# A decoder trunk on one core: both parts of x in one MLP product, and the first norm's high parts straight from the transposed bank

## The chip, the core and the metric

The kernel runs on one core of one Trainium2 chip. The metric is the device time of one execution in microseconds (us). One execution is profiled; its trace gives the rows below. Engines: TensorE (PE; its weight loads are PEld), VectorE (DVE), ScalarE (ACT), GpSimd (POOL) and SyncE (SP), which issues most transfers.

## What is computed

Two layers (`DEPTH = 2`) over 256 rows of 1024 columns, all in float32. The mixer (three groups of attention heads and gates) is untouched by the change. What is touched is the norm ahead of the first layer and the MLP:

```python
h = _layer_norm(x, ln_in_g, ln_in_b)
for l in range(DEPTH):
    mix = _hybrid_mixer(h, ...)
    h = _layer_norm(ALPHA * h + mix, ln1_g[l], ln1_b[l])
    ffn = _conv_gated_mlp(h, w_up[l], conv_w[l], conv_b[l], w_down[l])
    h = _layer_norm(ALPHA * h + ffn, ln2_g[l], ln2_b[l])

def _conv_gated_mlp(x, w_up, conv_w, conv_b, w_down):   # D_FF = 2816
    gate, val = jnp.split(x @ w_up, 2, axis=-1)
    gate = causal_depthwise_conv(gate, conv_w) + conv_b  # width 3, along the rows
    return (jax.nn.silu(gate) * val) @ w_down
```

## The kernel before

**Products in two parts.** TensorE multiplies in the type fp32r. To keep float32 accuracy each operand is split into a high part (ScalarE copies it to fp32r) and a low part (VectorE subtracts the high part from the full value), and each product is three matmuls: high by high, low by high, high by low (`mm3`).

**Weights.** `Stream` brings the weights in the order of `stream_plan` through the SP queue into seven `raw` tiles; `split` makes of each piece a tile `hl` of two parts (16 buffers): ScalarE the high part, VectorE or GpSimd the low part. `take` and `free` hand the tiles to the products in order.

**Order.** All instructions are issued in the order in which the program is written (a manual schedule). `Tasks` holds generators for the side work; `tick`, called after nearly each group of matmuls, moves each one step on, and `refill` splits the next weight piece. `Clocks` keeps a rough model of the engines' times, and `ready` and `refill` decide by it, so that the order of the side work depends on the model. All instructions go through one helper; their line in the trace is L276 (L281 in the changed kernel).

**PSUM.** Four banks `acc` for accumulators and four banks `att` for the rest. `get_att` and `att` hand out the latter in a ring; `att_free` gives back in the order of the program.

**The start.** `first_norm(tb, ...)` runs for rows 0 to 127 (tb 0) and 128 to 255 (tb 1). For each half of the columns (q) TensorE transposes four blocks into one `att` bank, and VectorE multiplies by the gain and adds the bias in the bank (`gb` holds both, one column for each block of 128). `spins` are matmuls on a constant that keep TensorE running. Then `split_out` makes the high part hTh (ScalarE, a whole bank) and the low part hTl (VectorE, a whole bank). `unit_x_tbfirst` then computes the q projection, one block of rows after the other, `evac` copies its two `acc` banks with ScalarE, rotary passes of VectorE follow, and TensorE transposes the result.

**The MLP.** hT is two tiles, hTh and hTl, of 8 blocks by 256 columns. An up unit j makes 256 columns of the gate and 256 of the up half in two `att` banks, G and V: `unit_w` goes through 8 weight tiles of 512 columns with four times three matmuls of 256 columns each. `task_act` then convolves G (ScalarE `cv<-att,convp` with scale and bias, VectorE four passes that read the bank), applies Silu, multiplies with V (VectorE `cv<-cv,att`) and splits the result into `act`. Unit j=0 is computed by rows (`up0`) and transposed into its G and V by `task_first`. A down unit is 24 matmuls of 512 columns into four `acc` banks; the last two down units are done at the end, one block of rows after the other, with the norm of each half behind it (`ln_half`).

Of the kernel before, what the change touches and what calls it, by code (L numbers as in the profile page):

```python
# [76 lines left out]
def stream_plan():  # L77


    plan = []  # L80

    def add(n, kts, cols=512, k0=0):
        step = 2 if cols <= 512 else 1
        for k in range(k0, k0 + kts, step):
            plan.append((n, k, step, cols))

    add("bq", 8)
    add("g1", 8, NG1)
    for n in ("biq", "cq", "ck", "cv", "aq", "ak", "av"):
        add(n, 8)  # L90
    for b in (1, 0):
        for nh in range(2):
            add(f"gate{b}{nh}", 8)
            add(f"br{b}{nh}", 4)
    for nh in range(2):
        add(f"gate2{nh}", 8)
    for nh in range(2):
        add(f"br2{nh}", 4)
    for k0 in (0, 4):
        for nh in range(2):  # L100
            add(f"out{nh}", 4, 512, k0)
    downs = {j: [j - 1] for j in range(1, NPAIR)}
    downs[NPAIR - 2] = []
    downs[NPAIR - 1] = [NPAIR - 3, NPAIR - 2, NPAIR - 1]
    for j in range(NPAIR):
        add(f"up{j}", 8)
        for d in downs.get(j, []):
            add(f"down{d}", 2, 1024)
    return plan, downs


class Stream:


    def __init__(self, nc, ve, sc, clocks, flat, raw_pool, hl_pool, plan):
# [6 lines left out]
        for (_, _, kts, cols) in plan:  # L122
# [4 lines left out]
            w = 512 if cols >= 512 else cols  # L127
# [68 lines left out]
def part(x):  # L196

    return x.name + "low" if x.name[:2] == "hl" and x.offset % 1024 >= 512 else x.name
# [126 lines left out]
def tile_hybrid(ctx: ExitStack, tc: tile.TileContext, a: dict, out: bass.AP):  # L325
# [273 lines left out]
    def first_norm(tb, st, hT, flag):  # L599
# [13 lines left out]
        for q in range(2):  # L613
# [4 lines left out]
            v = bk.rearrange("p (k t) -> p k t", k=4)  # L618
            for i, f in enumerate((ALU.mult, ALU.add)):
                ve.tensor_tensor(v, v, gb[:, i, 4 * q:4 * q + 4].unsqueeze(2).broadcast_to([P, 4, P]), f)  # L620
        spins((9, 5)[tb])
        if tb:
            att_free(warm)
        for q, bk in enumerate(bks):
            split_out(hT[0][:, 4 * q:4 * q + 4, tb * P:(tb + 1) * P],
                      hT[1][:, 4 * q:4 * q + 4, tb * P:(tb + 1) * P],
                      bk.rearrange("p (k t) -> p k t", k=4))
            att_free(bk)
            if not tb and not q:
                W.split(gp)  # L630
# [64 lines left out]
    def unit_w(hT, bks):  # L695

        for k in range(KD):
            w = W.take()
            for i in range(4):
# [6 lines left out]
                if i % 2:  # L706
                    T.tick()
            W.free()
# [16 lines left out]
    def layer(l, hT, hflag):  # L725
# [524 lines left out]
        def task_act(j, G, V):  # L1250
# [10 lines left out]
            att_free(G)  # L1261
# [3 lines left out]
            att_free(V)  # L1265
# [17 lines left out]
        for j in range(NPAIR):  # L1283
# [3 lines left out]
            G, V = get_att(), get_att()  # L1287
            unit_w(hT1, [G, V])
            T.add(task_act(j, G, V))
# [18 lines left out]
        for tb in range(2):  # L1308
            ts = slice(tb * P, (tb + 1) * P)
            st = small([P, 2, 6], "bst")  # L1310
            for i, (nh, c0, c1) in enumerate(PIECES):
                W.hold = W.hold or nh == 1
                for d in (NPAIR - 2, NPAIR - 1):
                    T.until(lambda: d in acts)
                    for f in range(2):
                        w = ws[d, f, nh][:, :, c0:c1]
                        mm3(dacc[nh][tb][:, c0:c1], acts[d][:, 0, f, ts], acts[d][:, 1, f, ts],
                            w[:, 0, :], w[:, 1, :], False, d == NPAIR - 1 and f == 1)
                        if tb and c1 == 512:
                            W.free()  # L1320
                        if True:
                            T.tick()
                if not (tb and nh and l < DEPTH - 1):
                    ln_half(tb, nh, st, dacc[nh][tb], (c0, c1), i)
# [18 lines left out]
    for _ in range(3):  # L1343
# [35 lines left out]
def lay_out(inp):  # L1379
# [3 lines left out]
    for l in range(DEPTH):  # L1383
# [9 lines left out]
        for j in range(NPAIR):  # L1393
            mats[f"up{j}"] = np.concatenate([inp["w_up"][l][:, 256 * j:256 * j + 256],
                                             inp["w_up"][l][:, D_FF + 256 * j:D_FF + 256 * j + 256]], axis=1)
# [34 lines left out]
```

## Time and profile before

| | |
|---|---|
| runs | 913.07 us, median of 3 (912.96 to 913.5) |
| the profiled execution | 913.03 us; its span in the trace 911.2 us |
| mean granted clock of TensorE | 0.997 of 2.4 GHz |
| TensorE busy | 898.0 us, 99% of the span |
| VectorE busy | 652.1 us, 72% |
| ScalarE busy | 512.1 us, 56% |
| GpSimd busy | 46.4 us, 5% |
| read from HBM | 159.47 MB, 176 GB/s over the span |

The span runs from the first to the last event that the profiler took; the execution's own time is 1.8 us longer. Matmuls overlap their neighbours in a row, so the time of one is read from the starts of rows, not from the busy column.

### The profile page before, as it was taken

The page shows a single profiled execution, that of the slowest core. Times are in us where ns is not written, and L with a number is a line of the kernel's source. Part 1 is how long each engine was busy: PE and PEld are TensorE (multiplying, and loading weights), DVE is VectorE, ACT ScalarE, POOL GpSimd, SP SyncE. Part 2 cuts the span into 40 slices and gives each one's busy share as a digit, 9 for nine tenths or more (in the row PEclk, how much of TensorE's full clock was granted, in tenths as well). Part 3 has the DMA queues.
Part 4 walks back from the last instruction along what each step waited for, and adds up shares of the span by engine and source line. Part 5 has one row for each costly group of instructions (what it writes and reads, how often), then busy time and mean ns, then how long its engine had stood idle before and what let it go on. Part 6 is the DMA issues. An engine that isn't in the chain of part 4 may idle for free. (4 is left out here: it accounts for less than half of the span.)

```text
span 911.2 us, 14459 instructions
## 1 busy us (share of the span) xinstructions
PE 898.0 (99%) x5334; PEld 786.7 (86%) x5334; DVE 652.1 (72%) x1272; ACT 512.1 (56%) x1008; POOL 46.4 (5%) x65
## 2 busy tenths in 40 slices
PE   8999999999999999999999999999999999999996
PEld 5878998888888999999888789888888899999995
DVE  6789576966778766666787966775757876766655
ACT  5664766655527555555365556775554475555540
POOL 5100000011010000000000000000200100000000
PEclk9999999999999999999999999999999999999998
DMA  8736253867537665655453335566675376666501
GB/s 300 278 94 205 73 185 116 303 203 242 167 102 273 213 188 182 191 187 177 130 170 137 99 115 162 185 207 211 198 241 183 127 262 188 174 198 187 175 11 47
DMA packets 46680, 161.47 MB, mean 177 GB/s; under 512 B 5840, under 2 KB 6864, under 8 KB 46608
## 3 DMA queue, kind: packets, MB, share of 16 engines
q1 hardware_dynamic: 44208, 155.20, 52.7%
q0 software_dynamic: 1408, 4.98, 2.0%
q8 instruction: 42, 0.69, 0.3%
q10 hardware_dynamic: 992, 0.35, 0.2%
q14 instruction: 30, 0.25, 0.1%
HBM read 159.47 MB, written 1.05 MB: 176 GB/s over the span
## 5 line engine op out<-in xcount | busy, mean ns | idle before, releaser
L276 DVE TENSOR_TENSOR hl<-raw,hl 128x512 fp32r<-128x512 f32 (+1 forms) x580 | 388.4, 695 | 183.3 <-ACT hl L276 181.7
L276 ACT ACTIVATE hl<-raw 128x512 fp32r<-128x512 f32 (+1 forms) x584 | 347.5, 628 | 189.4 <-PE att L276 95.2
L276 PE MATMUL acc<-hl,hTh 128*128 128x512 f32 (+1 forms) x896 | 274.7, 388 | 2.4 <-ACT hTh L276 2.3
L276 PE MATMUL att<-hTh,hl 128*128 128x256 f32 x1280 | 231.5, 283 | 0.0
L276 PEld LDWEIGHTS att<-hTh,hl 128*128 128x128 f32 x1280 | 200.8, 192 | 1.4
L276 PEld LDWEIGHTS acc<-hl,hTh 128*128 128x128 f32 x896 | 166.5, 188 | 38.8 <-ACT hTh L276 4.5
L276 PE MATMUL att<-hTl,hl 128*128 128x256 f32 x640 | 181.1, 283 | 0.0
L276 PE MATMUL acc<-hl,hTl 128*128 128x512 f32 (+1 forms) x448 | 164.8, 385 | 0.1
L276 PE MATMUL acc<-hl,act 128*128 128x512 f32 x528 | 123.1, 390 | 0.0
L276 PEld LDWEIGHTS att<-hTl,hl 128*128 128x128 f32 x640 | 122.8, 192 | 0.0
L276 PEld LDWEIGHTS acc<-hl,act 128*128 128x128 f32 x528 | 98.0, 188 | 19.6
L276 PEld LDWEIGHTS acc<-hl,hTl 128*128 128x128 f32 x448 | 83.9, 188 | 17.0 <-DVE hTl L276 1.8
L276 PE MATMUL acc<-hl,oT 128*128 128x512 f32 x288 | 68.4, 391 | 0.0
L276 PEld LDWEIGHTS acc<-hl,oT 128*128 128x128 f32 x288 | 53.6, 188 | 10.8
L276 DVE SCALAR_TENSOR_TENSOR cv<-att,convp,cv 128x255 f32<-128x255 f32 x88 | 40.4, 479 | 16.1 <-ACT cv L276 14.5
L276 PE MATMUL acc<-hTh,hl 128*128 128x256 f32 x256 | 48.0, 288 | 0.0
L276 PE MATMUL acc<-hl,mT 128*128 128x512 f32 x192 | 44.9, 391 | 0.0
L276 PEld LDWEIGHTS acc<-hl,mT 128*128 128x128 f32 x192 | 35.7, 188 | 7.2
L276 PEld LDWEIGHTS acc<-hTh,hl 128*128 128x128 f32 x256 | 39.8, 191 | 1.5 <-issue 1.3
L276 PE MATMUL acc<-hTl,hl 128*128 128x256 f32 x128 | 36.2, 283 | 0.0
L276 POOL TENSOR_TENSOR rs<-mv,mhalf 128x1 f32<-128x1 f32 x10 | 9.5, 948 | 485.0 <-DVE mv L276 485.0
L276 ACT ACTIVATE t<-acc 128x512 f32<-128x512 f32 (+1 forms) x36 | 20.1, 586 | 21.6 <-PE acc L276 20.8
(166 smaller groups left out, 680.3 us busy)
## 6 DMA issues: line engine op xcount, KB each, us to landing
raw<-in_w_dram SPq DMA_DIRECT2D x284, 512.0 KB, 4.2
raw<-in_w_dram SPq DMA_DIRECT2D x8, 332.0 KB, 4.0
lng<-in_ln_g_dram POOLq DMA_DIRECT2D x4, 512.0 KB, 4.4
lnb<-in_ln_b_dram POOLq DMA_DIRECT2D x4, 512.0 KB, 6.3
h<-in_x_dram SPq DMA_DIRECT2D x4, 256.0 KB, 4.2
lng<-in_ln_in_g_dram SPq DMA_DIRECT2D x1, 512.0 KB, 7.7
lnb<-in_ln_in_b_dram SPq DMA_DIRECT2D x1, 512.0 KB, 8.8
wu<-in_w_ukv_dram POOLq DMA_DIRECT2D x2, 256.0 KB, 5.3
```

The source lines that it names most:

```text
L276: f(*args, **kw)
```

## The change

**MLP.** hT becomes one tile of [128, 8, 2, 256], so that the high and low parts of a block lie side by side. `unit_w2` runs, for each weight block, one matmul of 512 columns (high weight by both parts) and one of 256 (low weight by the high part) into the left half of the bank. The two halves of a bank are then added: `task_sum` copies the left half to SBUF with ScalarE (tile `gv`) and adds the right half with VectorE. A bank now holds 128 columns of the gate or of the up half, so a unit is two halves (f = 0, 1) with two banks each, and the weights of `up{j}` (j from 1) are laid out in two pieces `up{j}.0` and `up{j}.1` of four blocks by 256 columns. `task_act` reads `gv` instead of the banks. Unit j=0 and the down units keep their form.

**First norm.** VectorE's two passes over the bank and the split are replaced: for each block of 128 columns ScalarE makes the high part straight from the bank, with gain and bias as scale and bias of the same instruction, and VectorE makes the full value from the bank; behind the four blocks VectorE subtracts once. The spins go from 9 and 5 to 3 and 3; of the weight splits at the start, two (before three) come ahead and two (before one) stand between the two banks.

**End of a layer.** The last sixteen weight tiles are taken pair by pair (d outer, halves of the columns inner) instead of half by half.

The diff, cut:

```diff
     def new_hT():
-        return (hp.tile([P, KD, S], R32, name=nm("hTh"), tag="hTh"),
-                hp.tile([P, KD, S], R32, name=nm("hTl"), tag="hTl"))
+        t = hp.tile([P, KD, 2, S], R32, name=nm("hT"), tag="hT")
+        return t[:, :, 0, :], t[:, :, 1, :], t
...
             transpose4(bk, h[tb][q])
-            v = bk.rearrange("p (k t) -> p k t", k=4)
-            for i, f in enumerate((ALU.mult, ALU.add)):
-                ve.tensor_tensor(v, v, gb[:, i, 4 * q:4 * q + 4].unsqueeze(2).broadcast_to([P, 4, P]), f)
-        spins((9, 5)[tb])
+        spins((3, 3)[tb])
         if tb:
             att_free(warm)
         for q, bk in enumerate(bks):
-            split_out(hT[0][:, 4 * q:4 * q + 4, tb * P:(tb + 1) * P],
-                      hT[1][:, 4 * q:4 * q + 4, tb * P:(tb + 1) * P],
-                      bk.rearrange("p (k t) -> p k t", k=4))
+            full = t2([P, 4, P])
+            for k in range(4):
+                i = 4 * q + k
+                g, b = gb[:, 0, i:i + 1], gb[:, 1, i:i + 1]
+                sc.activation(hT[0][:, i, tb * P:(tb + 1) * P], bk[:, k * P:(k + 1) * P], AF.Identity,
+                              bias=b, scale=g)
+                ve.tensor_scalar(full[:, k, :], bk[:, k * P:(k + 1) * P], g, b, ALU.mult, ALU.add)
             att_free(bk)
+            ks = slice(4 * q, 4 * q + 4)
+            ve.tensor_tensor(hT[1][:, ks, tb * P:(tb + 1) * P], full,
+                             hT[0][:, ks, tb * P:(tb + 1) * P].bitcast(F32), ALU.subtract)
             if not tb and not q:
-                W.split(gp)
+                for _ in range(2):
+                    W.split(gp)
...
+    def unit_w2(hT, bks):
+        for k in range(0, KD, 2):
+            w = W.take()
+            for kk in range(2):
+                for i in range(2):
+                    c = kk * 256 + i * P
+                    mm(bks[i], w[:, 0, c:c + P], hT[2][:, k + kk, :, :], k + kk == 0, False)
+                    mm(bks[i][:, 0:S], w[:, 1, c:c + P], hT[0][:, k + kk, :], False, k + kk == KD - 1)
+                T.tick()
+            W.free()
...
+        def task_pair(j, gv, done):
+            while len(done) < 2:
+                yield
+            yield from task_act(j, gv[:, 0, :], gv[:, 1, :], False)
+
+        def task_sum(gv, f, bks, done):
+            yield from ready("ACT", *bks)
+            for q, bk in enumerate(bks):
+                o = gv[:, q, f * S:f * S + S]
+                sc.activation(o, bk[:, 0:S], AF.Copy)
+                ve.tensor_tensor(o, o, bk[:, S:], ALU.add)
+                att_free(bk)
+            done.append(f)
...
-            G, V = get_att(), get_att()
-            unit_w(hT1, [G, V])
-            T.add(task_act(j, G, V))
+            gv = t4([P, 2, 512], n="gv")
+            done = []
+            for f in range(2):
+                bks = [get_att(), get_att()]
+                unit_w2(hT1, bks)
+                T.add(task_sum(gv, f, bks, done))
+            T.add(task_pair(j, gv, done))
...
-            for i, (nh, c0, c1) in enumerate(PIECES):
-                W.hold = W.hold or nh == 1
-                for d in (NPAIR - 2, NPAIR - 1):
-                    T.until(lambda: d in acts)
+            for d in (NPAIR - 2, NPAIR - 1):
+                T.until(lambda: d in acts)
+                for nh in range(2):
+                    W.hold = W.hold or (nh == 1 and d == NPAIR - 1)
...
-    for _ in range(3):
+    for _ in range(2):
         W.split(gp)
```

How the order of instructions changes is shown at three places. In the rows that follow, names carry the number of their tile: `hl8` is the ninth weight tile, `att_8` a bank of the pool; a name with its own number behind it is only its identity. What a row waits for stands in brackets.

**First place: ScalarE in the norm of rows 0 to 127, at the start of the program.** `hT` and `hTh` are the transposed rows, `raw` the weights as loaded. Before:

```order
L276 ACTIVATE hl0_175<-raw0_106 128x512 [waits DMAHW6_49]
L276 ACTIVATE hl1_178<-raw0_106 128x512
L276 ACTIVATE hl2_183<-raw1_108 128x512 [waits DMAHW7_49]
L276 ACTIVATE hTh_2_162<-att_8_186 128x4x128 [waits DVE_49,PE_49]
L276 ACTIVATE hl3_211<-raw1_108 128x512
L276 ACTIVATE hTh_2_162<-att_9_193 128x4x128 [waits DVE_49,PE_49]
```

And now:

```order
L281 ACTIVATE hl0_174<-raw0_106 128x512 [waits DMAHW6_49]
L281 ACTIVATE hl1_177<-raw0_106 128x512
L281 ACTIVATE hT_2_162<-att_7_182,gb_97 128x128 [waits DMAHW2_49,PE_49]
L281 ACTIVATE hT_2_162<-att_7_182,gb_97 128x128 [waits DVE_49] x3
L281 ACTIVATE hl2_205<-raw1_108 128x512 [waits DMAHW7_49]
L281 ACTIVATE hl3_208<-raw1_108 128x512
L281 ACTIVATE hT_2_162<-att_8_187,gb_97 128x128 [waits PE_49]
L281 ACTIVATE hT_2_162<-att_8_187,gb_97 128x128 [waits DVE_49] x3
```

Each copy of a whole bank has become four pieces of 128 columns; the second to fourth of a bank wait for VectorE, and the splits of `raw1` stand between the two banks.

VectorE at the same place (`bst` are the stats of rows 128 to 255). Before:

```order
L276 TENSOR_TENSOR att_8_186<-att_8_186,gb_97 128x512 [waits DMAHW2_49,PE_49]
L276 TENSOR_TENSOR att_8_186<-att_8_186,gb_97 128x512 [waits DVE_49]
L276 TENSOR_TENSOR att_9_193<-att_9_193,gb_97 128x512 [waits PE_49]
L276 TENSOR_TENSOR att_9_193<-att_9_193,gb_97 128x512 [waits DVE_49]
L276 TENSOR_TENSOR hTl_3_163<-att_8_186,hTh_2_162 128x4x128 [waits Activation_49]
L276 TENSOR_TENSOR hTl_3_163<-att_9_193,hTh_2_162 128x4x128 [waits Activation_49]
L276 BN_STATS bst_5_165<-h10_92 128x6 [waits DMAHW0_49]
```

And now:

```order
L281 TENSOR_SCALAR t2_9_195<-att_7_182,gb_97 128x128 [waits DMAHW2_49,Activation_49]
L281 TENSOR_SCALAR t2_9_195<-att_7_182,gb_97 128x128 [waits Activation_49] x3
L281 TENSOR_TENSOR hT_2_162<-t2_9_195,hT_2_162 128x4x128 [waits DVE_49]
L281 TENSOR_SCALAR t2_10_213<-att_8_187,gb_97 128x128 [waits Activation_49] x4
L281 TENSOR_TENSOR hT_2_162<-t2_10_213,hT_2_162 128x4x128 [waits DVE_49]
L281 BN_STATS bst_4_164<-h10_92 128x6 [waits DMAHW0_49]
L281 BN_STATS bst_4_164<-h11_93 128x6 [waits DMAHW1_49]
```

Four passes over whole banks have become eight pieces of 128 columns, each of which waits for ScalarE, and the subtraction for the low part follows each group of four.

**Second place: ScalarE ahead of the copy of the q projection** (`t4<-acc`), in layer 0. Before:

```order
L276 ACTIVATE hl13_366<-raw6_121 128x332
L276 ACTIVATE hl14_372<-raw7_181 128x332 [waits DMAHW0_49]
L276 ACTIVATE hl15_376<-raw7_181 128x332
L276 ACTIVATE t4_18_382<-acc_14_268 128x512
L276 ACTIVATE t4_18_382<-acc_15_269 128x512 [waits PE_49]
L276 ACTIVATE hl16_411<-raw8_214 128x512 [waits DMAHW1_49,Activation_49]
```

And now:

```order
L281 ACTIVATE hl14_386<-raw7_180 128x332 [waits DMAHW0_49]
L281 ACTIVATE hl15_390<-raw7_180 128x332
L281 ACTIVATE hl16_396<-raw8_211 128x512 [waits DMAHW1_49,PE_49,Activation_49]
L281 ACTIVATE hl17_400<-raw8_211 128x512 [waits PE_49,Activation_49]
L281 ACTIVATE t4_21_405<-acc_15_273 128x512
L281 ACTIVATE t4_21_405<-acc_16_274 128x512 [waits PE_49]
```

The two splits of `raw8` now stand ahead of the two copies; before they stood behind them.

**Third place: TensorE in up unit j=1 of layer 0.** `att_257` and `att_258` (now `att_260` and `att_261`) are the gate and up banks of unit j=0, the others those of unit j=1, `hl170` to `hl173` its weight tiles. Before, at its third and fourth weight tile:

```order
L276 MATMUL att_256_2923<-hTh_237_2705,hl170_2832 128x256 x2
L276 MATMUL att_256_2923<-hTl_238_2706,hl170_2832 128x256
L276 MATMUL att_256_2923<-hTh_237_2705,hl170_2832 128x256 x2
L276 MATMUL att_256_2923<-hTl_238_2706,hl170_2832 128x256
L276 MATMUL att_255_2922<-hTh_237_2705,hl171_2859 128x256
L276 MATMUL att_255_2922<-hTh_237_2705,hl171_2859 128x256 [waits DVE_49]
L276 MATMUL att_255_2922<-hTl_238_2706,hl171_2859 128x256
L276 MATMUL att_255_2922<-hTh_237_2705,hl171_2859 128x256 x2
```

And now, at the change from its first half to its second:

```order
L281 MATMUL att_258_2937<-hT_240_2720,hl171_2873 128x512
L281 MATMUL att_258_2937<-hT_240_2720,hl171_2873 128x256
L281 MATMUL att_259_2938<-hT_240_2720,hl171_2873 128x512
L281 MATMUL att_259_2938<-hT_240_2720,hl171_2873 128x256
L281 MATMUL att_263_3001<-hT_240_2720,hl172_2882 128x512 [waits DVE_49,PE_49,Activation_49]
L281 MATMUL att_263_3001<-hT_240_2720,hl172_2882 128x256
L281 MATMUL att_264_3002<-hT_240_2720,hl172_2882 128x512 [waits DVE_49]
L281 MATMUL att_264_3002<-hT_240_2720,hl172_2882 128x256
```

Before, the unit kept to its two banks to its end; now it changes to two other banks half-way, the first matmul into each of them with a wait.

## Rows read from the trace of the kernel before

**Rows 1.** The page's busy line: engine, busy us, share, instructions.

```profile
PE 898.0 (99%) x5334; PEld 786.7 (86%) x5334; DVE 652.1 (72%) x1272; ACT 512.1 (56%) x1008; POOL 46.4 (5%) x65
```

**Rows 2.** Windows: stretch, us, busy of PE, PEld, DVE, ACT, POOL; clock, DMA, GB/s.

```profile
0.00:20.00 20.00, 16.85 (x71) 9.61 (x72) 13.79 (x30) 9.04 (x14) 11.00 (x23) 1.00 0.89 317
...
300.00:400.00 100.00, 100.00 (x710) 94.41 (x709) 64.77 (x106) 55.75 (x94) 0.00 (x0) 1.00 0.60 186
```

**Rows 3.** TensorE's timeline, layer 0's MLP: start, us, engine, line, operation, tiles, shapes.

```profile
298.97 0.40 PE L276 MATMUL att<-hTh,hl 128*128 128x256 f32 x2
...
310.48 5.63 PE L276 MATMUL acc<-hl,act 128*128 128x512 f32 x24
315.95 0.40 PE L276 MATMUL att<-hTh,hl 128*128 128x256 f32 x2
```

**Rows 4.** Timeline, ScalarE and VectorE at one gate bank; in brackets idle time before.

```profile
326.94 1.02 ACT L276 ACTIVATE cv<-att,convp 128x256 f32<-128x256 f32 x2
...
328.00 1.91 DVE L276 SCALAR_TENSOR_TENSOR cv<-att,convp,cv 128x255 f32<-128x255 f32 x4 [0.42 <-ACT cv L276]
...
330.00 0.63 ACT L276 ACTIVATE cv<-cv 128x512 f32<-128x512 f32 x1 [0.32 <-DVE cv L276]
```

**Rows 5.** Groups by form, ScalarE: count, busy us, mean ns, idle before.

```profile
L276 ACT ACTIVATE cv<-att,convp 128x256 f32<-128x256 f32 x44 | 22.5, 562 | 7.9 <-PE att L276 6.3
...
L276 ACT ACTIVATE p<-att,smx 128x256 f32<-128x256 f32 x24 | 11.2, 490 | 4.2 <-DVE smx L276 4.2
...
L276 ACT ACTIVATE p<-att,smx 128x128 f32<-128x128 f32 x24 | 8.5, 372 | 12.1 <-DVE smx L276 12.1
...
L276 ACT ACTIVATE oc<-att,rina 128x128 f32<-128x128 f32 x16 | 5.7, 366 | 1.9 <-ACT hl L276 1.4 <-PE att L276 0.5
```

**Rows 6.** Groups by form, VectorE.

```profile
L276 DVE SCALAR_TENSOR_TENSOR cv<-att,convp,cv 128x255 f32<-128x255 f32 x44 | 21.0, 478 | 14.5 <-ACT cv L276 14.5
...
L276 DVE TENSOR_SCALAR p<-p,rinv 128x256 f32<-128x256 f32 x16 | 4.9, 350 | 0.3
...
L276 DVE COPY q<-att 128x512 f32<-128x512 f32 x6 | 4.1, 687 | 2.8 <-PE att L276 2.8
...
L276 DVE TENSOR_SCALAR p<-p,rinv 128x128 f32<-128x128 f32 x16 | 3.5, 282 | 0.1
...
L276 DVE CAST chr<-att 16x256 fp32r<-16x256 f32 x2 | 0.8, 412 | 0.1
...
L276 DVE TENSOR_SCALAR m<-cst 128x256 f32<-128x256 f32 x1 | 0.3, 284 | 0.0
```

**Rows 7.** Timeline of the start, all engines.

```profile
7.00 1.15 ACT L276 ACTIVATE hl<-raw 128x512 fp32r<-128x512 f32 x2 [3.05 <-DMA raw<-in_w_dram]
...
7.92 2.77 DVE L276 TENSOR_TENSOR att<-att,gb 128x512 f32<-128x512 f32 x4 [0.29 <-PE att L276]
...
10.10 1.19 PE L276 MATMUL acc<-hl,hTh 128*128 128x512 f32 x4
...
10.59 1.51 DVE L276 TENSOR_TENSOR hTl<-att,hTh 128x512 fp32r<-128x512 f32 x2
...
12.01 1.28 DVE L276 BATCH_NORM_STATS2 bst<-h 128x6 f32<-128x512 f32 x2
...
17.25 2.76 DVE L276 TENSOR_TENSOR att<-att,gb 128x512 f32<-128x512 f32 x4 [1.04 <-PE att L276]
...
20.10 0.60 ACT L276 ACTIVATE hTh<-att 128x512 fp32r<-128x512 f32 x1 [0.73 <-DVE att L276]
...
26.75 1.06 ACT L276 ACTIVATE t<-acc 128x512 f32<-128x512 f32 x2
...
29.57 1.06 PE L276 MATMUL att<-ident,t 128*128 128x128 f32 x8
```

**Rows 8.** Timeline, layer 1: first matmul of unit j=1, product of unit j=0.

```profile
726.57 0.40 PE L276 MATMUL att<-hTh,hl 128*128 128x256 f32 x2
...
733.85 0.69 DVE L276 TENSOR_TENSOR cv<-cv,att 128x512 f32<-128x512 f32 x1 [0.84 <-ACT cv L276]
```

More of the change, by code (lines that the diff above doesn't have):

```diff
@@ L82, in add @@
     def add(n, kts, cols=512, k0=0):
-        step = 2 if cols <= 512 else 1
+        step = {256: 4, 1024: 1}.get(cols, 2)
         for k in range(k0, k0 + kts, step):
@@ L126, in __init__ @@
             off += P * n
[L127 removed]
+            w = 512 if cols in (256, 512, 1024) else cols
             for q in range(n // w):
@@ L196, in part @@
 def part(x):
-    return x.name + "low" if x.name[:2] == "hl" and x.offset % 1024 >= 512 else x.name
+    n = {"hl": 1024, "hT": 512}.get(x.name[:2])
+    return x.name + "low" if n and x.offset % n >= n // 2 else x.name
 class Clocks:
@@ L1248, in layer, with task_act @@
         bc_load(lnb, a["ln2_b"], D, l * D)
-        def task_act(j, G, V):
+        def task_pair(j, gv, done):
[10 more added lines that the diff above has]
+            done.append(f)
+        def task_act(j, G, V, banks=True):
             yield from ready("ACT", G)
@@ L1260, in task_act @@
                 ve.scalar_tensor_tensor(c[:, f, 2:256], g[:, 0:254], cw(f, 0), c[:, f, 2:256], ALU.mult, ALU.add)
-            att_free(G)
+            if banks:
+                att_free(G)
             yield from ready("ACT", c)
@@ L1264, in task_act @@
             ve.tensor_tensor(c, c, V.rearrange("p (f t) -> p f t", f=2), ALU.mult)
-            att_free(V)
+            if banks:
+                att_free(V)
             yield from ready("ACT", c)
@@ L1286, in layer @@
                 continue
-            G, V = get_att(), get_att()
-            unit_w(hT1, [G, V])
-            T.add(task_act(j, G, V))
+            gv = t4([P, 2, 512], n="gv")
+            done = []
+            for f in range(2):
+                bks = [get_att(), get_att()]
+                unit_w2(hT1, bks)
+                T.add(task_sum(gv, f, bks, done))
+            T.add(task_pair(j, gv, done))
             if j in downs and downs[j] and dacc is None:
@@ L1393, in lay_out @@
         for j in range(NPAIR):
-            mats[f"up{j}"] = np.concatenate([inp["w_up"][l][:, 256 * j:256 * j + 256],
-                                             inp["w_up"][l][:, D_FF + 256 * j:D_FF + 256 * j + 256]], axis=1)
+            gate, up = (inp["w_up"][l][:, o + 256 * j:o + 256 * j + 256] for o in (0, D_FF))
+            mats[f"up{j}"] = np.concatenate([gate, up], axis=1)
+            for f in range(2):
+                mats[f"up{j}.{f}"] = np.concatenate([gate[:, P * f:P * f + P], up[:, P * f:P * f + P]], axis=1)
             mats[f"down{j}"] = inp["w_down"][l][256 * j:256 * j + 256, :]
```

20 lines of the change are left out of this document (11 added, 9 removed).

## The prediction, made before the result was known

> **What bounds the kernel now.** I read the busy line of the page first, then the table by stages, then the timeline of TensorE. TensorE is busy for 898.0 of 911.2 us [rows 1]; from 300 to 400 us it has no idle time at all, while VectorE is busy for 64.8 and ScalarE for 55.8 of those 100 us [rows 2]. The only stage where TensorE stands still for long is the start: 16.85 busy in the first 20 us, and part of that is spins. So the time is TensorE's row of instructions plus what it waits for at the start, and a change is worth what it does to these two. The profiled execution took 913.03 us for a span of 911.2; the sum is made against 913.03, which is 0.04 under the median of the runs, 913.07. A measurement of this kernel can tell about 0.2% (1.8 us) from no change, so "same" is 911.2 to 914.9.
>
> **The MLP product.** An up unit of before is 96 matmuls of 256 columns. They start at 298.97 and the down unit behind them at 310.48 [rows 3]: 11.51 us, 0.120 each. The 24 matmuls of 512 columns of the down unit take from 310.48 to 315.95, 0.228 each. A new unit is 32 of 512 and 32 of 256 columns: 32 x 0.228 + 32 x 0.120 = 11.13 us. The columns are the same; what goes is 32 starts. 0.38 us a unit, ten units a layer, two layers: **7.6 us gained**, and it counts in full because TensorE is the bound there. The rows put 0.013 to 0.015 us on each start beside the columns' own time at the 2.4 GHz level (granted clock 1.00, [rows 2]). The Trainium skill ("TensorE: Matmul & The Clock Gate", Back-to-back issue gap) gives the isolated gap as columns divided by 2.4 plus 2.5 ns; by that the 32 starts of a unit would be worth 0.08 us and the whole only 1.6. This trace's gaps are 120 and 228 ns where the page has 109 and 216, so the rows decide; the page's case is the last rival below.
>
> The two halves of a bank must now be added: per unit four ScalarE copies and four VectorE sums of 128x256. From both sides they cost at most 0.56 and 0.48 us each [rows 5, 6], 2.2 and 1.9 us in a step of 17.0 us [rows 3], so ScalarE goes from 56 to some 69% and VectorE from 65 to some 76%. Both stay under TensorE, and a pair of banks is freed one product ahead of its next use. In the new order ScalarE has split the weight tile 12 to 15 places ahead when it comes to a copy that waits for TensorE, so a late copy has over 10 us of cover. I cost them at nothing; without that cover they are the third rival.
>
> **A wait that is new in the MLP.** Unit j=1 now fills two banks, then two others, and all four of the pool are taken: two by its first half, two by the gate and up banks of j=0. At the third place of the changed order the second bank of the second half waits for VectorE. Banks come free in order, so this is the up bank of j=0, whose last reader is the product cv<-cv,att. In the trace that product ends at 733.85 + 0.69 = 734.54, 7.97 us after the first matmul of the unit at 726.57 [rows 8]. The second half reaches that bank after 16 x 0.348 (first half, a pair of 0.228 and 0.120 each) + 8 transposes of 0.09 (estimate from the 0.36 between rows of four) + 0.35 = 6.64 us. TensorE stands for 7.97 - 6.64 = 1.3 us, or 1.2 since the transposes come 0.1 earlier. Before, the unit wrote two banks only and no one waited. Everything of the MLP is queued behind it on TensorE. Two layers: **2.5 us lost** (2.4 to 2.7).
>
> **The first norm.** Before, VectorE applies gain and bias to a transposed bank in four passes (7.92 + 2.77, [rows 7]), ScalarE copies each bank in one instruction, VectorE takes the low part. Now it is ScalarE and VectorE "beside" each other on the same bank, in pieces of 128 columns. The first place of the changed order shows that they don't run beside each other: every VectorE piece waits for ScalarE, and the second to fourth ScalarE piece of a bank wait for VectorE. They take turns. The trace has such a case: VectorE's first pass over a gate bank needs only the first half of cv, but starts at 328.00, when ScalarE has left the bank with both halves (326.94 + 1.02, [rows 4]). The Trainium skill ("PSUM — Partial Sum Buffer", PSUM bank collisions raise a hardware error) has it as a rule that no two engines may be on one bank at once, reads included, and that speaks against this edit; without it the first bank would cost four ScalarE pieces alone, the second rival.
>
> The price of one turn. ScalarE, 128x128 with per-row scale and bias: no row has it. cv<-att,convp is that at 128x256, 562 ns; from 256 to 128 columns p<-att,smx falls by 490 - 372 = 118; so 0.45 us [rows 5]. VectorE, 128x128 out of PSUM with two per-row operands: PSUM sources cost 687 ns for 512 and 412 for 256 columns, so about 275 for 128, and an operand adds 350 - 284 = 66, twice: 0.41 us [rows 6]. Handing over: 0.04 to VectorE (327.96 to 328.00) and 0.09 back at most (329.91 to 330.00, [rows 4]); I take 0.09 for both. A turn is **0.95 us**. Ends: 0.366 + 0.282 + 0.07 = 0.72 (one operand each, the second from SBUF), and 0.562 + 0.478 + 0.13 = 1.17 (256 columns each). I stay at 0.95, as it is built from the forms nearest to the new ones.
>
> Now the start, step by step [rows 7]. Rows 0 to 127: ScalarE is free at 7.00 + 1.15, so the first piece starts at 8.1; the fourth ends at 8.1 + 3 x 0.95 + 0.45 = 11.4. Two splits stand between the banks: 12.4 (1.15, overlapping a little). Four turns of the second bank: 16.2; the low part (1.51 for two): 16.9. That is where VectorE began the stats of rows 128 to 255 at 12.01 before, so **4.9 us late**; that chain itself is unchanged. Rows 128 to 255: the first transposed bank was ready at 17.25, now 22.15. Four turns: 25.95; low part: 26.7; the second bank's first ScalarE piece is done by then, VectorE's ends at 27.15, and the last ScalarE piece at 27.15 + 2 x 0.95 + 0.45 = 29.5. Before it was 20.10 + 0.60: **8.8 us late**. Behind it ScalarE has the table loads and eight splits as before (one now ahead of the loads), but also two splits ahead of the copy of the q unit (second place of the changed order): 1.1 more. So that copy ends 9.9 later than 26.75 + 1.06, the rotary passes of VectorE follow, and TensorE's transposes of the result, at 29.57 before, start near 39.5. They stand at the same place in TensorE's row, which has nothing left ahead of them by about 36.6, so TensorE waits for them. From there it is dense and gives nothing back: **9.9 us lost**. The dropped spins and the third and fourth split that moved into the norm cost nothing, since TensorE waits there anyway. There are 13 turns on this chain: with the ends of a turn 6.9 to 12.8.
>
> The last sixteen tiles of a layer are now taken pair by pair instead of half by half. The tail of the kernel hangs on the end of the first block's products and on VectorE behind it; both keep their place. The activation of the last pair gets 1.4 us more before it is needed. I cost it at nothing; it covers the 1.2 us by which the sums make that chain longer.
>
> **Sum.** 913.03 - 7.6 + 2.5 + 9.9 = **917.8 us**. With the short turn 913.03 - 7.6 + 2.4 + 6.9 = 914.7, with the long one 920.9.
>
> **Rivals.**
> 1. Turns at the low end: 914.7, about no change. For it: ScalarE pieces follow each other closely and both short forms exist as rows. Against: both new forms have two operands and a PSUM source. Not slower from a turn of 0.73 us down.
> 2. No turns on the chip's time scale (the change as it reads): ScalarE makes four pieces in about 4 x 0.37 us, the first matmul comes near 8.6 instead of 10.10, and the start gains 1.5: 913.03 - 1.5 - 7.6 + 2.5 = 906.4, faster. Against it stand the waits in the order and the row at 328.00.
> 3. The sums become a bound: if TensorE waits 0.5 us in each of 20 units for a bank or an activation, 917.8 + 10 = 927.8. Decides where VectorE passes some 95% in the MLP; I get 76.
> 4. A matmul start costs less between mixed widths: with 1.6 instead of 7.6 gained, 923.8. Against it are two widths measured at the same price per start.
>
> **How the numbers follow.** Forecast 0.74, rivals 0.12, 0.05, 0.05, 0.04. The range goes from 913.6 (low turn and a wait in the MLP of half its size) to 921.6 (long turn, and some ten matmuls behind the sparse start at 0.30 each, as the four at 10.10, instead of 0.228: 0.7). Below it are rival 2 and a little of 1, above it rivals 3 and 4 and the forecast's tail. Faster: rival 2 and a little more, 0.06. Same: rival 1 and the forecast's low edge, 0.13. Slower: 0.81.
>
> **What would show it.** The profile after should have ScalarE pieces hT<-att,gb alternating with VectorE pieces t<-att,gb, some 0.95 us from one ScalarE piece to the next; the transposes of the q unit near 39.5; up units with 11.13 us from first matmul to the next unit; a gap of TensorE of about 1.2 us some 6.6 us into each layer's unit j=1; VectorE near 76% from 300 to 400 us. If the pieces of ScalarE stand under 0.5 us apart, or the up unit stays at 11.5, the step named is wrong.

## The result and the profile after

The changed kernel takes 923.91 us, median of four runs (922.45 to 925.36); before took 913.02 beside it. The ratio is 1.0118, with an interval of 1.0106 to 1.013: slower by 10.9 us where 4.8 were forecast, and above the range, which ended at 921.6. The profiled execution took 925.36 us, 12.3 more than that of before, with a span of 923.6. The four runs lie in two pairs, near 922.6 (mean granted clock 0.994 and 0.995) and near 925.2 (0.992 and 0.993), and the profiled one is of the upper pair; what sets the pair isn't settled. The busy line of its page:

```profile
PE 900.4 (97%) x4686; PEld 755.3 (82%) x4686; DVE 683.2 (74%) x1360; ACT 541.7 (59%) x1100; POOL 46.8 (5%) x65
```

TensorE has 2.4 us more of busy time than before [rows 1] although it has 648 matmuls fewer (640 of the MLP and 8 spins), and its span is 12.4 us longer, so most of the loss is idle time. The windows tell where (columns as in [rows 2]):

```profile
0.00:20.00 20.00, 13.87 (x44) 7.39 (x45) 9.58 (x25) 8.99 (x17) 6.38 (x10) 0.91 0.78 266
20.00:40.00 20.00, 16.05 (x69) 11.60 (x67) 12.84 (x32) 14.63 (x29) 8.01 (x24) 0.91 0.65 205
38.00:40.00 2.00, 0.14 (x1) 0.00 (x0) 1.97 (x8) 2.00 (x5) 0.00 (x0) 1.00 0.96 250
40.00:42.00 2.00, 1.52 (x10) 1.56 (x11) 2.00 (x4) 0.95 (x3) 0.00 (x0) 0.81 0.90 352
42.00:44.00 2.00, 2.00 (x9) 2.00 (x9) 1.26 (x3) 2.00 (x5) 0.00 (x0) 0.50 1.02 414
44.00:46.00 2.00, 2.00 (x13) 2.00 (x13) 1.97 (x4) 1.05 (x3) 0.00 (x0) 0.83 1.03 377
300.00:400.00 100.00, 99.02 (x518) 84.07 (x517) 77.49 (x139) 67.33 (x125) 0.00 (x0) 1.00 0.65 196
```

The start has lost TensorE's busy time, and there is something that the forecast had only as a tail: from 42 to 44 us TensorE is busy all the time at a granted clock of 0.50, its 1.2 GHz level, after standing nearly still from 38 to 40. In the trace of before the clock is 1.00 in each of these stretches. In the MLP VectorE is at 77 and ScalarE at 67%, as worked out (76 and 69), and TensorE has one gap of 0.98 in 100 us.

The norm of rows 0 to 127, ScalarE's timeline and then VectorE's (start, us, engine; idle time before in brackets):

```profile
8.41 1.15 ACT L281 ACTIVATE hl<-raw 128x512 fp32r<-128x512 f32 x2 [4.46 <-DMA raw<-in_w_dram]
9.47 0.44 ACT L281 ACTIVATE hT<-att,gb 128x128 fp32r<-128x128 f32 x1
10.39 0.46 ACT L281 ACTIVATE hT<-att,gb 128x128 fp32r<-128x128 f32 x1 [0.48 <-DVE t L281]
11.33 0.46 ACT L281 ACTIVATE hT<-att,gb 128x128 fp32r<-128x128 f32 x1 [0.48 <-DVE t L281]
12.26 0.46 ACT L281 ACTIVATE hT<-att,gb 128x128 fp32r<-128x128 f32 x1 [0.48 <-DVE t L281]
```

```profile
9.94 0.41 DVE L281 TENSOR_SCALAR t<-att,gb 128x128 f32<-128x128 f32 x1 [2.55 <-ACT hT L281]
10.88 0.41 DVE L281 TENSOR_SCALAR t<-att,gb 128x128 f32<-128x128 f32 x1 [0.53 <-ACT hT L281]
11.82 0.41 DVE L281 TENSOR_SCALAR t<-att,gb 128x128 f32<-128x128 f32 x1 [0.53 <-ACT hT L281]
```

The two engines take turns: 9.47 to 9.91 is ScalarE, 9.94 to 10.35 VectorE, 10.39 ScalarE again, 0.92 to 0.94 us from one ScalarE piece to the next. The forecast had 0.95, made of 0.45, 0.41 and 0.09. The weights landed later than in the trace of before (ScalarE starts at 8.41, not at 7.00 [rows 7]), which no part of the change explains: over all the traces here this start lies between 7.00 and 8.08 with the old norm and between 6.42 and 8.41 with the new. What the change does is to make the norm hang on it: ScalarE's first piece stands right behind the splits of these weights (9.47).

TensorE's timeline shows what becomes of that:

```profile
13.29 8.21 PE L281 MATMUL acc<-hl,hT 128*128 128x512 f32 x20 [1.90 <-ACT hl L281]
27.75 10.39 PE L281 MATMUL acc<-hl,hT 128*128 128x512 f32 x47 [0.68 <-DVE hT L281]
40.48 1.21 PE L281 MATMUL att<-ident,t 128*128 128x128 f32 x8 [2.33 <-DVE t L281]
...
115.95 4.58 PE L281 MATMUL acc<-hT,hl 128*128 128x256 f32 x36
120.80 0.38 PE L281 MATMUL acc<-hT,hl 128*128 128x256 f32 x1 [0.28 <-ACT hl L281]
121.53 5.18 PE L281 MATMUL acc<-hT,hl 128*128 128x256 f32 x41 [0.34 <-DVE hl L281]
...
281.94 5.75 PE L281 MATMUL acc<-hl,hT 128*128 128x512 f32 x24 [0.25 <-ACT hT L281]
...
296.98 4.83 PE L281 MATMUL att<-hT,hl 128*128 128x512 f32 x26
302.79 5.56 PE L281 MATMUL att<-hT,hl 128*128 128x512 f32 x30 [0.98 <-DVE cv L281]
308.18 5.67 PE L281 MATMUL acc<-hl,act 128*128 128x512 f32 x24
313.69 11.45 PE L281 MATMUL att<-hT,hl 128*128 128x512 f32 x64
324.98 5.67 PE L281 MATMUL acc<-hl,act 128*128 128x512 f32 x24
330.48 11.45 PE L281 MATMUL att<-hT,hl 128*128 128x512 f32 x64
```

The transposes of the q unit start at 40.48, 10.9 us later than in [rows 7], and TensorE waits 2.33 us for them. The first products of the MLP's rows start at 281.94; the same row of before is this one:

```profile
268.30 1.20 PE L276 MATMUL acc<-hl,hTh 128*128 128x512 f32 x4 [0.25 <-ACT hTh L276]
```

So 13.6 us are lost by then, 2.7 of them after the transposes. From there on the kernel gains only 1.3. An up unit takes 324.98 - 313.69 = 11.29 us (11.13 forecast, 11.51 before), a down unit 5.50 (5.47 before); the step of both is 16.79 where [rows 3] has 16.98. The wait in unit j=1 is there as forecast. Its bracket shows 0.98 us, but a bracket counts from the end that the profile gives the matmul before, and in a dense row that end lies behind the next start (308.18 + 5.67 is past 313.69); what a wait costs is read from starts, in e5.

### The profile page after: what moved, and what is told of

Same layout as the page of the kernel before. It is cut to its first block, busy times and chain, and to the rows that moved or that the text cites. A ratio compares the mean times of both kernels' runs of the same rounds, so it can differ in the third digit from the quotient of the medians.

```text
span 923.6 us, 13372 instructions
## 1 busy us (share of the span) xinstructions
PE 900.4 (97%) x4686; PEld 755.3 (82%) x4686; DVE 683.2 (74%) x1360; ACT 541.7 (59%) x1100; POOL 46.8 (5%) x65
## 5 line engine op out<-in xcount | busy, mean ns | idle before, releaser
L281 PE MATMUL acc<-hl,hT 128*128 128x512 f32 (+1 forms) x1344 | 318.1, 392 | 7.4 <-ACT hT L281 4.3
L281 PEld LDWEIGHTS acc<-hl,hT 128*128 128x128 f32 x1344 | 249.8, 191 | 64.1 <-ACT hT L281 7.6
L281 PE MATMUL att<-hT,hl 128*128 128x512 f32 (+1 forms) x1280 | 230.3, 340 | 2.0 <-DVE cv L281 2.0
L281 PEld LDWEIGHTS att<-hT,hl 128*128 128x128 f32 x1280 | 197.3, 188 | 32.7 <-DVE cv L281 2.6
L281 PE MATMUL acc<-hT,hl 128*128 128x256 f32 x384 | 50.0, 286 | 0.6 <-DVE hl L281 0.3
L281 PEld LDWEIGHTS acc<-hT,hl 128*128 128x128 f32 x384 | 47.1, 191 | 2.5 <-issue 1.3
L281 ACT ACTIVATE gv<-att 128x256 f32<-128x256 f32 x80 | 29.0, 383 | 21.8 <-PE att L281 21.8
L281 DVE SCALAR_TENSOR_TENSOR cv<-gv,convp,cv 128x255 f32<-128x255 f32 x80 | 36.8, 481 | 1.5
L281 DVE TENSOR_TENSOR gv<-gv,att 128x256 f32<-128x256 f32 x80 | 30.7, 421 | 9.1 <-ACT gv L281 5.2
L281 ACT ACTIVATE p<-att,smx 128x128 f32<-128x128 f32 (+1 forms) x48 | 19.7, 431 | 21.1 <-DVE smx L281 21.1
```

What stands on the lines that cost most here:

```text
L281: f(*args, **kw)
```

## The experiments

The theory in the trace's terms: (N) the loss is the start's, (T) the turns on one bank make it, (C) TensorE's lower clock behind the long wait adds to it, (B) the two bank waits cost their full length. Four more, S, K, L and I, are about the price of mixed widths and are named where they are tested. Changes of a few tenths of a us are compared by the ratio to the runs of before on the same chip, whose median went from 913.07 to 913.56.

**e1: the MLP part without the new norm.**

```diff
-        spins((3, 3)[tb])
+        spins((9, 5)[tb])
...
-                sc.activation(hT[0][:, i, tb * P:(tb + 1) * P], bk[:, k * P:(k + 1) * P], AF.Identity,
-                              bias=b, scale=g)
-                ve.tensor_scalar(full[:, k, :], bk[:, k * P:(k + 1) * P], g, b, ALU.mult, ALU.add)
+            split_out(hT[0][:, 4 * q:4 * q + 4, tb * P:(tb + 1) * P],
+                      hT[1][:, 4 * q:4 * q + 4, tb * P:(tb + 1) * P],
+                      bk.rearrange("p (k t) -> p k t", k=4))
...
```

> The changed kernel with the norm, the spins and the splits of the start as before: the MLP part and the end of the layer alone. Theory N (the start holds the whole loss; in the trace the MLP of the changed kernel gains 0.66 us in layer 0 and 0.58 in layer 1, as TensorE's starts shift from +13.64 to +12.98 and +12.40): 913.0 - 1.2 = 911.8 us, between 911.0 and 912.6. Rival M (the sums of the MLP also take from the start or the mixer, 2.7 us of which lie between the first transposes and the MLP): 914 to 916.

Measured: 911.53 us, ratio 0.9982 (0.9973 to 0.9991). The MLP part and the end of the layer gain 1.5 us, within the 0.2% that the forecast called no change; rival M falls.

**e2: the norm part alone,** in the kernel before.

```diff
-        spins((9, 5)[tb])
+        spins((3, 3)[tb])
...
+                sc.activation(hT[0][:, i, tb * P:(tb + 1) * P], bk[:, k * P:(k + 1) * P], AF.Identity,
+                              bias=b, scale=g)
+                ve.tensor_scalar(full[:, k, :], bk[:, k * P:(k + 1) * P], g, b, ALU.mult, ALU.add)
...
```

> The kernel before with the new norm, its spins and its splits alone. Theory N: 923.9 + 1.2 = 925.1 us (up to 926.6, as in the profiled execution), the transposes of the q unit near 40.5. Rival M: below 922, the rest of the loss being the MLP's.

Measured: 925.61 us, ratio 1.0134 (1.012 to 1.0148). The norm part loses 12.5 us; with the 1.5 of e1 that is 11.0, the whole change's 10.9, so N holds. The transposes of the q unit stand not near 40.5, as expected here, but where the forecast had put them, near 39.5; the first weights are split at 7.46 in this trace:

```profile
7.46 1.15 ACT L276 ACTIVATE hl<-raw 128x512 fp32r<-128x512 f32 x2 [3.50 <-DMA raw<-in_w_dram]
...
39.51 1.07 PE L276 MATMUL att<-ident,t 128*128 128x128 f32 x8 [2.23 <-DVE t L276]
```

**e3: the same pieces, grouped by engine.** ScalarE's and VectorE's own rows are the same as in the changed kernel; only the waits between them differ.

```diff
                 sc.activation(hT[0][:, i, tb * P:(tb + 1) * P], bk[:, k * P:(k + 1) * P], AF.Identity,
                               bias=b, scale=g)
+            for k in range(4):
+                i = 4 * q + k
+                g, b = gb[:, 0, i:i + 1], gb[:, 1, i:i + 1]
                 ve.tensor_scalar(full[:, k, :], bk[:, k * P:(k + 1) * P], g, b, ALU.mult, ALU.add)
```

> The changed kernel, but in the norm ScalarE makes its four pieces of a bank first and VectorE its four pieces behind them; each engine's own order of instructions stays word for word the same, only who waits for whom changes. Theory T (the price is the turns on one bank): two hand-overs a bank in place of eight; the low part of rows 0 to 127 ends 2.3 us earlier, ScalarE's last piece some 6 us earlier, the transposes of the q unit near 34.5; 923.9 - 6 = 917.9 us, 916 with TensorE's clock kept up there. Rival P (the pieces themselves, sixteen of ScalarE and sixteen of VectorE, are what costs): 922 to 924.

Measured: 916.53 us, ratio 1.0034 (1.0022 to 1.0047), 7.4 us less than the changed kernel. ScalarE's timeline:

```profile
7.86 1.15 ACT L281 ACTIVATE hl<-raw 128x512 fp32r<-128x512 f32 x2 [3.90 <-DMA raw<-in_w_dram]
8.91 1.49 ACT L281 ACTIVATE hT<-att,gb 128x128 fp32r<-128x128 f32 x4
10.29 1.15 ACT L281 ACTIVATE hl<-raw 128x512 fp32r<-128x512 f32 x2
11.32 1.51 ACT L281 ACTIVATE hT<-att,gb 128x128 fp32r<-128x128 f32 x4
```

VectorE's and TensorE's:

```profile
10.44 1.37 DVE L281 TENSOR_SCALAR t<-att,gb 128x128 f32<-128x128 f32 x4 [3.14 <-ACT hT L281]
...
12.87 1.37 DVE L281 TENSOR_SCALAR t<-att,gb 128x128 f32<-128x128 f32 x4
```

```profile
12.91 7.64 PE L281 MATMUL acc<-hl,hT 128*128 128x512 f32 x20 [0.92 <-DVE hT L281]
20.39 1.04 PE L281 MATMUL att<-ident,h 128*128 128x128 f32 x8
...
34.01 1.07 PE L281 MATMUL att<-ident,t 128*128 128x128 f32 x8 [0.42 <-DVE t L281]
```

Four pieces of ScalarE take 1.5 us in a row, four of VectorE 1.4, where four turns took 3.7. T holds: most of the price is the turns, and P, by which it is the pieces, falls. The transposes come 34.01 - 7.86 = 26.2 us behind the first split, where the changed kernel has 40.48 - 8.41 = 32.1; with a wait of 0.42 ahead of them in place of 2.33 the granted clock stays at 1.00 from 36 to 48 us, and the way from them to the MLP's first products is 1.5 shorter, 7.4 in all. VectorE is on the second bank (12.87) when ScalarE has left it (12.83), and on the first when ScalarE has left that.

**e4: constant matmuls where TensorE waits.**

```diff
                 bk = yield from att()
+                if l == 0 and key == "qbT" and tb == 0:
+                    for _ in range(9):
+                        nc.tensor.matmul(bk, spin, spin.unsqueeze(1).broadcast_to([P, 4, P]), start=True, stop=True,
+                                         skip_group_check=True)
                 transpose4(bk, s[:, tb, :])
```

> The changed kernel with nine constant matmuls (0.22 us each) in TensorE's row right ahead of the first transposes of the q unit, where it stands still for 2.3 us. Theory C (TensorE falls to the 1.2 GHz level behind that wait, from 41 to 45 us, and that is 1.5 us of the 2.7 lost between these transposes and the MLP): clock 1.00 from 40 to 46 us, 922.4 us, and runs closer together than the 2.9 us of the changed kernel. Rival: the clock there is not the cause, 923.9 and the same spread.

Measured: 922.22 us (921.99 to 922.63), ratio 1.01 (1.0084 to 1.0115), 1.6 us under the changed kernel's by the ratios, whose intervals overlap; the traces decide. Its four runs lie 0.6 us apart, those of the changed kernel 2.9. Windows of e4, then rows of ScalarE and TensorE:

```profile
40.00:42.00 2.00, 2.00 (x15) 2.00 (x14) 1.36 (x3) 2.00 (x5) 0.00 (x0) 1.00 1.03 420
42.00:44.00 2.00, 2.00 (x14) 1.88 (x13) 2.00 (x5) 2.00 (x5) 0.00 (x0) 1.00 1.02 397
```

```profile
7.09 1.15 ACT L281 ACTIVATE hl<-raw 128x512 fp32r<-128x512 f32 x2 [3.14 <-DMA raw<-in_w_dram]
```

```profile
39.13 1.07 PE L281 MATMUL att<-ident,t 128*128 128x128 f32 x8 [0.44 <-DVE t L281]
...
279.01 5.74 PE L281 MATMUL acc<-hl,hT 128*128 128x512 f32 x24 [0.25 <-ACT hT L281]
```

The clock stays at 1.00, and from the transposes (39.13) to the MLP's first products (279.01) the kernel now loses 1.1 us against before, not 2.7. The 1.6 between them is C's. The 1.1 are two waits for weight parts, shown above near 120 us in the changed kernel: their brackets add up to 0.6, but by starts the first delays the row by 120.80 - (115.95 + 36 x 0.120) = 0.5 and the second by 0.73 - 0.12 = 0.6. All traces with the new norm have these two waits (e2, e3, e4, e7), before and e1 don't; which of its edits brings them wasn't tested.

**e7: e3 with the spins of before.**

```diff
-        spins((3, 3)[tb])
+        spins((9, 5)[tb])
```

> The kernel of e3 (pieces grouped by engine) with nine and five spins in the norm as before in place of three and three. Theory C (in e3 the first products run at the 1.2 GHz level, 0.37 us each, because TensorE stood still before them, and the transposes of rows 128 to 255 queue behind them at 20.39 although their rows were ready at 19.43): the transposes come about 1 us earlier, 915.5 us. Rival: the row of products isn't what the transposes wait for, 916.5 or, by the longer spins, 917.

Measured: 915.33 us, ratio 1.0021 (1.0012 to 1.003), against 1.0034 for e3: the spins were worth some 1.2 us there, though the two intervals overlap. In the traces the transposes stand 25.4 us behind the first split, 0.7 less than in e3. Even grouped and with all spins, the new norm is 3.6 us slower than the old one in e1 (0.9982).

**e5: the banks of unit j=0 given back at once.**

```diff
-            yield from task_act(0, G, V)
+            gv = t4([P, 2, 512], n="gv")
+            yield from ready("ACT", G)
+            sc.activation(gv[:, 0, :], G, AF.Copy)
+            att_free(G)
+            ve.tensor_copy(gv[:, 1, :], V)
+            att_free(V)
+            yield from task_act(0, gv[:, 0, :], gv[:, 1, :], False)
```

> The kernel of e1 (MLP part with the old norm), but the gate and up banks of unit j=0 are copied out at once (ScalarE the gate, VectorE the up half, 512 columns each) and given back, so that the second half of unit j=1 finds free banks. Theory B (the two waits of 0.97 us for VectorE's product of j=0 are lost in full): 911.5 - 1.9 = 909.6 us and no idle time of TensorE in unit j=1. Rival: another reader or the copies end last there, 911.5 and an idle time at the same place.

Measured: 909.48 us, ratio 0.9956 (0.9943 to 0.9968); against e1's ratio that is 2.4 us, more than the 1.9 expected from the brackets. TensorE's row of the unit, without a wait:

```profile
283.42 10.14 PE L281 MATMUL att<-hT,hl 128*128 128x512 f32 x56
293.39 5.63 PE L281 MATMUL acc<-hl,act 128*128 128x512 f32 x24
```

From 283.42 to the down unit are 9.97 us, where the changed kernel takes 308.18 - 296.98 = 11.20 for the same 56 matmuls. So each wait costs 1.2 us, as forecast, and the two 2.5: B holds, with the length taken from starts.

**e6, e10 and e11: the order of the widths.** All are e1 with the up unit's matmuls in another order. The changed kernel alternates 512 and 256; e6 runs 512, 512, 256, 256 on alternating banks:

```diff
                 for i in range(2):
                     c = kk * 256 + i * P
                     mm(bks[i], w[:, 0, c:c + P], hT[2][:, k + kk, :, :], k + kk == 0, False)
+                for i in range(2):
+                    c = kk * 256 + i * P
                     mm(bks[i][:, 0:S], w[:, 1, c:c + P], hT[0][:, k + kk, :], False, k + kk == KD - 1)
```

> The kernel of e1, but in the up unit the two matmuls of 512 columns stand in a row, then the two of 256, so that the width changes half as often. A pair costs 0.3528 us in the changed kernel where 0.228 + 0.120 = 0.348 was forecast. Theory S (the change of width costs 2.4 ns each time): a unit falls from 11.29 to 11.21 us, 20 units give 1.6 us, 909.9. Rival (the 512 columns of the two-part tile cost 0.233 by themselves, or the alternation between banks counts): the unit stays at 11.29, 911.5 us.

Measured: 908.14 us, ratio 0.9941 (0.9929 to 0.9953). TensorE's rows:

```profile
300.19 11.30 PE L281 MATMUL att<-hT,hl 128*128 128x512 f32 x64
311.33 5.61 PE L281 MATMUL acc<-hl,act 128*128 128x512 f32 x24
316.78 11.30 PE L281 MATMUL att<-hT,hl 128*128 128x512 f32 x64
```

The unit is at 11.14, the price forecast from the rows of before (11.13), and the step at 16.59. S, by which half the changes of width leave the unit at 11.21, misses: half of them gone, the whole surplus is gone. Neither the two-part tile nor the width of 512 makes the unit dearer than forecast; alternating the widths does. e10 does the same with all four matmuls on one bank:

```diff
-            for kk in range(2):
-                for i in range(2):
+            for i in range(2):
+                for kk in range(2):
                     c = kk * 256 + i * P
                     mm(bks[i], w[:, 0, c:c + P], hT[2][:, k + kk, :, :], k + kk == 0, False)
+                for kk in range(2):
+                    c = kk * 256 + i * P
                     mm(bks[i][:, 0:S], w[:, 1, c:c + P], hT[0][:, k + kk, :], False, k + kk == KD - 1)
```

> The kernel of e1 with the up unit in the order 512, 512, 256, 256 columns, all four on one bank, and then the same on the other. e6 (the same widths, banks alternating) took the unit from 11.29 to 11.135 us, twice what half the changes of width would give at 2.4 ns each. Theory S (only the order of the widths counts): unit 11.13, 908.1 us. Rival K (what counts is that a matmul of 256 columns follows straight on the bank and columns that the one of 512 has just written): the second of the two 256 and the first are two matmuls behind their 512, so this also gives 11.13. Rival L (what counts is the alternation of banks from one matmul to the next): unit 11.29 or more, 911.5.

Measured: 907.27 us, ratio 0.9933 (0.9919 to 0.9946), the unit again at 11.14. So it isn't the alternation of banks, and rival L falls; what e10 has over e6 is a shorter bank wait in unit j=1 (bracket 0.67 in place of 1.13). e11 keeps most changes of width but never puts a 256 right behind the 512 of its own weight block (`low` is the matmul of 256 columns):

```diff
...
+            for n, (kk, i) in enumerate(xs):
+                c = kk * 256 + i * P
+                mm(bks[i], w[:, 0, c:c + P], hT[2][:, k + kk, :, :], k + kk == 0, False)
+                if n:
+                    low(*xs[n - 1])
...
+            low(*xs[3])
```

> The kernel of e1 with the 256-column matmul of each pair put one pair behind, within a weight tile: 512, 512, 256, 512, 256, 512, 256, 256. e6 and e10 took the unit from 11.29 to 11.135 us with half the changes of width, whatever the bank. Theory I (a 256-column matmul that stands alone between two of 512 costs 5 ns; there are 32 a unit in the changed kernel, none in e6 and e10): here 16 of 32 stand alone, unit 11.21 us, 909.9 us. Rival K (it costs only where the 256 follows on the 512 of its own weight block): unit 11.13, 908.1 us. Rival S (2.4 ns for every change of width, and the rest of e6 and e10 is something else): 48 changes in place of 64, unit 11.25, 910.7 us.

Measured: 911.3 us, ratio 0.9976 (0.9967 to 0.9986):

```profile
300.99 11.45 PE L281 MATMUL att<-hT,hl 128*128 128x512 f32 x64
312.28 5.62 PE L281 MATMUL acc<-hl,act 128*128 128x512 f32 x24
317.74 11.45 PE L281 MATMUL att<-hT,hl 128*128 128x512 f32 x64
```

The unit stays at 11.29, the step is 16.75. K (11.13) falls, and I (11.21) and S (11.25) miss the unit too. With widths in pairs the extra 0.2 us of a step is gone, with three quarters of the changes left 0.16 stays; neither count gives both, and what in TensorE takes the time stays open.

**e8: the end of the layer as before,** on e1.

```diff
-            for d in (NPAIR - 2, NPAIR - 1):
-                T.until(lambda: d in acts)
-                for nh in range(2):
+            for i, (nh, c0, c1) in enumerate(PIECES):
+                W.hold = W.hold or nh == 1
+                for d in (NPAIR - 2, NPAIR - 1):
+                    T.until(lambda: d in acts)
...
```

> The kernel of e1 with the end of the layer as before (half by half instead of pair by pair). Forecast that the order costs nothing and covers the longer chain of the last unit by 1.4 us: without it TensorE waits at most 0.2 us a layer for the last pair's activation, 911.5 to 911.9 us. Rival (the new order is needed for the gain): over 912.5, with an idle time of TensorE ahead of the last pair's products.

Measured: 912.68 us, ratio 0.9991 (0.9982 to 1.0), against e1's 0.9982: 0.8 us dearer, with intervals that overlap. TensorE's timeline at the end of layer 0:

```profile
440.81 7.38 PE L281 MATMUL acc<-hl,act 128*128 128x512 f32 x31
448.49 9.61 PE L281 MATMUL acc<-hl,act 128*128 128x512 f32 x41 [0.30 <-DVE act L281]
```

The stretch lasts until 457.93, 17.12 us, where e1 takes 16.35 (440.00 to 456.35) without a wait. The last activation is late when its products stand second, as the cover worked out in the forecast said, but by 0.8 us in layer 0 and nothing in layer 1; 911.5 to 911.9 was too low.

**e9: e5 and e6 together.** The diffs are those two.

> The MLP part with the old norm, with the banks of j=0 given back early (as in e5) and the two widths in rows of two (as in e6) together. If the two gains are separate: 911.5 - 2.0 - 3.4 = 906.1 us; idle time in unit j=1 of 1.13 us gone and the unit at 11.13. If the earlier second half only meets another wait there: 907 to 908.

Measured: 905.3 us, ratio 0.9912 (0.9898 to 0.9925): 8.3 us faster than before on the same chip, and the fastest version here. The two gains add up: by the ratios 2.4 of e5 and 3.7 of e6 on e1's 1.6 make 7.8, and e9 has 8.0. The rows of unit j=1 and the next step:

```profile
283.65 10.02 PE L281 MATMUL att<-hT,hl 128*128 128x512 f32 x56
293.50 5.61 PE L281 MATMUL acc<-hl,act 128*128 128x512 f32 x24
298.95 11.30 PE L281 MATMUL att<-hT,hl 128*128 128x512 f32 x64
```

## Why the prediction was wrong

The direction and the mechanisms of the three terms in the sum were right. One of them, the products, came out at half its size, and a term that the sum had at nothing, the way from the transposes to the MLP, cost 2.7. Against the profiled execution, terms in us (the products as 20 steps of 16.79 in place of 16.98, the bank wait by starts as in e5):

| term | forecast | measured in the trace |
|---|---|---|
| products of the MLP, up and down | -7.6 | -3.8 |
| bank wait in unit j=1, two layers | +2.5 | +2.5 |
| start, to the transposes of the q unit | +9.9 | +10.9 |
| from there to the MLP | 0 (0.7 in the range) | +2.7 |
| ends of the layers | 0 | 0 |
| sum | +4.8 | +12.3 |

**The MLP product is the step that failed most.** The price of a start was taken from rows in which all matmuls have one width, 0.120 and 0.228, and added for a row in which the widths alternate. The pair costs 11.29 / 32 = 0.353 there, and the down unit behind it 0.03 more. In the order of e6, with the widths in pairs, the forecast's own 11.13 comes out and the step gains 0.39 (0.38 forecast). So the term was mis-sized by the order, half of it lost; the unit came out between the 11.13 that the forecast named as its sign and the 11.5 that it named against it. What in TensorE takes the time stays open (e11). The rival of a cheaper start had the direction but not the reason: the starts that go are worth what the rows said. That its 923.8 lies next to the measured 923.91 is luck: it takes 6.0 from the products, where 3.8 were missing, and has nothing for the 2.7 behind the transposes. The Trainium skill ("TensorE: Matmul & The Clock Gate", Back-to-back issue gap) has an isolated gap from which a pair comes to an estimated (512 + 256) / 2.4 + 5 = 325 ns, and says of it that in a stream the weight loads count too. The traces show 348 at best and 353 in alternation, so the measurement decides here.

**The first norm** held nearly to the letter: a turn of 0.94 (0.95), pieces of 0.456 and 0.410 (0.45 and 0.41), the transposes at 39.51 and 39.13 in e2 and e4 (39.5). The further 1.0 of the profiled execution of the changed kernel comes with weights that landed 1.4 later than in [rows 7]. In the three traces with turns the transposes stand at a fixed distance behind the first split: 7.09 and 39.13, 7.46 and 39.51, 8.41 and 40.48, each 32.0 to 32.1; with the old norm it is 22.0 to 23.1, not fixed. From 7.00 that gives 39.06, 9.5 us late where the forecast had 9.9, and the other 1.4 of the 10.9 are the late weights, for which the forecast's start from 7.00 had no room. e3 shows that it is mostly the turns: the same rows with fewer hand-overs are 7.4 us faster. That the dropped spins cost nothing wasn't tested with the turns; in the grouped form they were worth 0.7 to 1.2 (e7). The rule of the Trainium skill that the forecast weighed ("PSUM — Partial Sum Buffer", PSUM bank collisions raise a hardware error) fits the traces: in the rows shown no two pieces are on one bank at a time, and the rival that needs them side by side, 906.4, fell. The waits stand in the program, though, so no run here shows what the chip does with two engines on one bank.

**"From there it is dense and gives nothing back"** was the other step that failed: dense it is but for two short waits, but TensorE comes out of a wait of 2.33 us, and its clock is 0.50 from 42 to 44. The forecast had put such a cost of 0.7 into the upper end of the range, at the sparse start, and not behind the long wait that it had itself worked out (36.6 to 39.5). e4 prices it at 1.6. The two waits for weight parts near 120 us make the other 1.1; they come with the new norm (e2 has them, e1 not).

**The rest.** The bank wait: 1.2 by starts against 1.2 to 1.3, and e5 gives it back in full. The sums cost nothing, as forecast (VectorE at 77%), and the end of the layer covers the longer chain; without the new order e8 loses 0.8.

## What to carry to other kernels

In this kernel two engines that share one PSUM bank in small pieces run one after the other and pay a hand-over each time, so count turns and not pieces; group all of one engine's pieces of a bank ahead of the other's. Here even that stayed 3.6 us behind the passes over whole banks, so the old norm with the new MLP (e9) is the version to keep. Work that is queued behind the first transfer takes over its lateness, as the transposes did here at a fixed 32 us. A price per matmul from rows of one width holds for that order only: where widths are mixed, put equal widths together. A wait of the bounding engine that a change creates costs more than its length, if the engine comes out of it at a lower clock; a few matmuls on constants in the gap bought that back here. The idle time in brackets reads too short for TensorE: the bank wait shown as 0.98 cost 1.2, so compare starts.

## What the runs showed of the hardware

- Matmuls of 512 and 256 columns in alternation cost 353 ns a pair; in the order 512, 512, 256, 256 they cost 348, on one bank or on two (e6, e10). With 512, 512, 256, 512, 256, 512, 256, 256 it is 353 again (e11).
- After 2.3 us with almost no work TensorE ran its next 332-column matmuls at a granted clock of 0.50 (42 to 44 us); with nine constant matmuls in that gap it stayed at 1.00 (e4).
- A ScalarE piece of 128x128 out of PSUM with per-row scale and bias takes 0.456 us alone (mean of the changed kernel), but four in a row take 1.49 (e3); for VectorE it is 0.410 and 1.37.
